# Ten instead of eight of sixteen k-tiles by seven products in the input projection of a decoder block

## The chip, the cores and the metric

The kernel runs on one core of a Trainium2 chip. The metric is the device time of one execution in microseconds. The kernel before takes 1338.32 us, the median of three runs (1338.11 to 1338.59).

## What is computed

One layer of a decoder for 256 rows of width 2048 in float32: a norm, one input projection, three kinds of causal attention over its q, k and v columns, three sigmoid gates, a branch projection, an output projection and a residual; then a second norm and a SwiGLU feed-forward part. Only the input projection is changed:

```python
h = rmsnorm(x, g_mix)                       # 256 x 2048
proj = h @ w_in                             # 2048 x 12288
qkv = proj[..., :3 * MIX_WIDTH]             # MIX_WIDTH = 2048: q, k, v
gates = jax.nn.sigmoid(proj[..., 3 * MIX_WIDTH:])   # three gates of 2048
...
merged = gates[0] * (o_a @ w_branch_a) + gates[1] * (o_b @ w_branch_b) + gates[2] * (o_c @ w_branch_c)
x = x + merged @ w_out
gu = rmsnorm(x, g_ffn) @ w_gu
x = x + (silu(gu[..., :D_FF]) * gu[..., D_FF:]) @ w_down
```

## The kernel before

**Three passes.** To keep float32's accuracy every factor is split into a rounded high part (type float32r) and the rest, its low part. `split` (L107 to L112) does this with a cast on ScalarE and a subtraction on VectorE. `product` (L169 to L174) multiplies with three matmuls: high by high (L172), high by low (L173), low by high (L174).

**Tiles.** The 256 rows are two halves t = 0 and 1 of 128. The 2048 inner columns are sixteen k-tiles of 128; four k-tiles make a chunk. Output columns come in blocks of 512. A weight block as it is loaded is 128 partitions x 2 k-tiles x 512 columns, 512 KB. One matmul covers one k-tile, one row half and 512 output columns.

**Units.** The projection's 24 column blocks are worked in units (L858): v block 0 and one gate block by the plain way (`project`), then eleven pairs of two column blocks A and B: four qk pairs, one vv, one vg and five gates pairs. Each pair is one call of `project_pair` (L351 to L424). In the text they are numbered 1 to 11.

**Seven products.** Chunks 0 and 1 (`WC`, eight k-tiles) are worked by a Strassen scheme with seven products in place of eight. The row halves and the halves of the chunk's k-tiles make the 2 x 2 blocks of the activations; the halves of the k-tiles (kh) and the columns A and B make those of the weights: b11 and b12 are the upper halves of A and B, b21 and b22 the lower ones. Forms 1, 2, 5, 6, 7, 3 and 4 are the seven products, summed into the PSUM tiles X, Y, Z and V. Sums of activations (forms 3, 5, 6, 7) are made once, by `sums_of_h`; `Both` holds them and hands out the operands. Sums of weights are made in each pair: u = b11 + b12 for form 5, then + b22 for form 6, then + b21 for form 4, and b12 + b22 for form 7. Some are VectorE additions (L344, `add_into` L333), some are DMAs issued on GpSimd that add into their target (L389, L395). With `by_dma`, in pairs 1 to 9, b12 + b22 is done by DMA; in pairs 10 and 11 VectorE does it.

**The plain rest.** The other eight k-tiles (chunks 2 and 3) are worked by `rest`: one 512 KB weight block, split, against both row halves, 12 matmuls. The list `ks` holds the four first k-tiles 8, 10, 12 and 14 of these blocks; each is used once for B (n = 1, into Z and V) and once for A (n = 0, into Y and X).

The order in a pair is forms 1, 2 and 5; two plain blocks of B; form 6; a plain block; form 7; a plain block; form 3; two plain blocks of A; form 4; two plain blocks; then the first splits of the next pair (`begin_pair`, L338). Seven forms of 12 matmuls and eight plain blocks of 12 make 180 matmuls. The snapshots s1, z5, x2 and x3 (L328) and the sums c22, c12 and c11 (L407, L408, L411, L423) put the outputs together.

**Buffers and order.** Split weights live in five slots each for high and low parts (`w_hi`, `w_lo` in the pool `wpool`). Raw blocks for forms live in the pool `gx` (`g_raw`, six slots), those for plain blocks in `w_raw` (four slots). Half-size tiles of 512 columns (`half_kb`) come from twelve slots `sc`. All weight loads are issued on SyncE in the order of the program (`fetch`). The tile framework orders the rest within each engine. With each split `parts` moves pending attention work on by a step (`advance`), so attention's instructions lie between those of the pairs. The last column block of the output projection and the gate-and-up projection go through `project_pair` too, with eight k-tiles by seven products.

Of the kernel before, what the change touches and what calls it, by code (L numbers as in the profile page):

```python
# [9 lines left out]
F32 = mybir.dt.float32  # L10
F32R = mybir.dt.float32r
# [7 lines left out]
P = 128  # L19
# [36 lines left out]
def hybrid_block(ctx: ExitStack, tc: tile.TileContext, x, w_in, w_branch, w_out, w_gu, w_down, rel_bias,  # L56
# [237 lines left out]
    class Both(Sums):  # L294


        def __init__(self, pl, cols, wc):
            super().__init__(pl, "b", wc, False)
            self.shared(pl)
            self.plain = cols.plain  # L300


    WC = (0, 1)

    def load(w, k, col0, pl=None):

        raw = pl.tile([P, 2, NB], F32, name="g_raw", bufs=6 if pl is gx else 4) if pl else wpool.tile([P, 2, NB], F32, name="w_raw", bufs=4)
        (nc.sync.dma_start if w is w_down else fetch)(raw, block(w, k, col0))
        return raw
# [16 lines left out]
    def snapshot(ps):  # L326
        sb = half_kb()
        nc.scalar.copy(sb, ps)  # L328
        return sb
# [5 lines left out]
    def quarter(acts, w, kh, col0):  # L335
        return [load(w, 4 * c + 2 * kh, col0, gx) for c in acts.wc]

    def begin_pair(acts, w, colA, colB):  # L338

        b11, b12 = (quarter(acts, w, 0, col0) for col0 in (colA, colB))  # L340
        p11 = [parts(b) for b in b11]
        u = [gx.tile([P, 2, NB], F32, name="u") for _ in acts.wc]
        for a, b, d in zip(b11, b12, u):
            nc.vector.tensor_add(d, a, b)  # L344
        b21 = quarter(acts, w, 1, colA)
        return p11, b12, u, b21, [parts(b) for b in (u if by_banks(w) else b21)]

    def by_banks(w):
        return w is w_gu or w is w_out

    def project_pair(acts, w, colA, colB, begun=None, nxt=None, by_dma=False, early=None):  # L351
# [6 lines left out]

        def form(ps, f, srcs, start, stop, split=False):
            for i, c in enumerate(acts.wc):  # L360
                wh, wl = srcs[i] if split else parts(srcs[i])
                for j in range(2):
                    product(ps, *acts.form(f, c, j), wh[:, j], wl[:, j], start and i + j == 0,
                            stop and i + j == len(acts.wc))

# [5 lines left out]

        ks = [k for c in range(KT // 4) if c not in acts.wc for k in (4 * c, 4 * c + 2)]
        p11, b12, u, b21, second = begun or begin_pair(acts, w, colA, colB)
        form(X, 1, p11, True, True, True)
        if by_banks(w):
            tc.keep_in_program_order(nc.scalar.copy(Y, X))
            form(Z, 5, second, True, True, True)
            doubled[:] = [tc.keep_in_program_order(nc.scalar.copy(V, Z))]
            form(Y, 2, b21, False, False)
        else:  # L380
            s1 = snapshot(X)
            form(Y, 2, second, True, False, True)
            form(Z, 5, u, True, True)
            z5 = snapshot(Z)
        plain = [load(w, k, colB) for k in ks[:2]]
        b22 = quarter(acts, w, 1, colB)
        if by_dma:
            for d, a in zip(b12, b22):
                nc.gpsimd.dma_start(d, a, accum_op=ALU.add)  # L389
        rest(1, ks[0], Z, V, start=not by_banks(w), raw=plain[0])  # L390
        rest(1, ks[1], Z, V, raw=plain[1])
        add_into(u, b22)
        form(X, 6, u, False, True)
        for d, a in zip(u, b21):
            nc.gpsimd.dma_start(d, a, accum_op=ALU.add)  # L395
        x2 = snapshot(X)
        rest(1, ks[2], Z, V)
        if not by_dma:
            add_into(b12, b22)
        form(X, 7, b12, False, True)  # L400
        x3 = snapshot(X)
        rest(1, ks[3], Z, V, stop=True)
        c22 = half_kb()
        if by_banks(w):
            nc.vector.tensor_sub(c22, V, x3)
        else:
            nc.vector.tensor_sub(z5, z5, x3)  # L407
            nc.vector.tensor_add(c22, V, z5)  # L408
        form(Z, 3, b22, False, True)
        c12 = half_kb()  # L410
# [3 lines left out]
        for k in ks[:2]:  # L414
            rest(0, k, Y, X)
        form(X, 4, u, False, False)
        for k in ks[2:]:
# [62 lines left out]
    for c in range(2, 4):  # L480
        whole[c] = gx.tile([P, NT, 4, P], F32, name="g_raw", bufs=6)
    columns = {c: [whole[c][:, t] for t in range(NT)] for c in range(4)}
# [103 lines left out]
    def load_rows():  # L586
        for t in range(NT):
            for n in range(2):
                rows.append(gx.tile([P, 2 * NB], F32, name="g_raw", bufs=6))
                fetch(rows[-1], x[t * P:(t + 1) * P, 2 * n * NB:2 * (n + 1) * NB])  # L590
                yield
# [297 lines left out]
    for (kind, what), after in zip(units, units[1:] + [(None, None)]):  # L889
# [46 lines left out]

    pgx.close()
    tc.keep_in_program_order(nc.scalar.preload_act_table_set("natural_log_exp_and_others"))
    m = Columns(pool(pm, "pm", "right"), "m", KT)
# [371 lines left out]
```

## Time and profile before

| | |
|---|---|
| median of three runs | 1338.32 us |
| the profiled execution | 1337.34 us |
| its span in the profile | 1335.6 us |
| DMA engines, mean | 266 GB/s |
| w_raw blocks of the input projection | 103 loads of 512 KB, 7.0 us to land |
| g_raw blocks of the input projection | 88 loads of 512 KB, 6.2 us to land |

The engines: PE is TensorE's matmuls, PEld its weight loads, DVE is VectorE, ACT ScalarE, POOL GpSimd, SP SyncE. Lines of the kernel are given as L108. A row of a timeline reads: start, duration, engine, line, operation, output and inputs with their shapes, number. In a table of windows each row has the stretch, its length, and for each engine busy time and the number of instructions, then the granted clock of TensorE, the share of the DMA engines and what they moved. A row of DMA issues ends with the KB of one and the median time from issue to landing. Windows of a pair are cut where VectorE starts c11 (L423), the last sum of a pair.

### The profile page before, as it was taken

Reading aid. Unit: us, or ns where it says so; the run is one execution under the profiler, and the core shown is the slowest. Engines: PE = TensorE matmul, PEld = TensorE weight load, DVE = VectorE, ACT = ScalarE, POOL = GpSimd, SP = SyncE. Lnnn points to the kernel's source line nnn. Section 1 sums busy time; section 2 is a strip of 40 time slices with the busy share of each in tenths; the row PEclk is TensorE's granted clock in tenths of the full one; section 3 lists DMA queues with packets and bytes.
Section 4 is the critical chain, followed back from the end, with each engine's and each line's share of the span. In section 5 each row is a group of like instructions: output and inputs, shape, how many; then the busy total and the mean of one; then the engine's idle time right before and its main releaser. Section 6 shows DMA issues by size and latency. Waiting matters only on the chain.

```text
span 1335.6 us, 17783 instructions
## 1 busy us (share of the span) xinstructions
PE 1328.6 (99%) x6243; PEld 1158.7 (87%) x6243; DVE 1168.9 (88%) x1254; ACT 940.9 (70%) x1209; POOL 130.9 (10%) x195
## 2 busy tenths in 40 slices
PE   9999999999999999999999999999999999999998
PEld 6888888888888888888888888888888888888887
DVE  7978898989888897986999999989899997998887
ACT  7786867788777776544777778777877875665563
POOL 1100110001111111100210000001000001001010
PEclk9999999999999999999999999999999999999999
DMA  9997878797788878877988889889899977789883
GB/s 359 308 282 246 263 210 258 252 277 223 263 267 282 277 241 289 294 249 244 305 312 267 259 265 278 238 252 308 279 286 274 281 216 253 252 276 301 270 271 96
DMA packets 119505, 354.70 MB, mean 266 GB/s; under 512 B 32832, under 2 KB 34552, under 8 KB 119416
## 3 DMA queue, kind: packets, MB, share of 16 engines
q1 hardware_dynamic: 77016, 277.45, 58.4%
q0 software_dynamic: 19984, 69.76, 22.2%
q10 hardware_dynamic: 22416, 6.36, 2.8%
q8 instruction: 49, 0.80, 0.2%
q14 instruction: 40, 0.33, 0.1%
HBM read 294.26 MB, written 14.70 MB: 231 GB/s over the span
## 4 chain that ended last, share of the span: by engine, by line
PE 98%; DMA 1%; ACT 0%; DVE 0%; SPq 0%; issue 0%; DVEq 0%
PE qs L172 12%; PE ps L173 12%; PE qs L174 12%; PE qs L173 12%; PE ps L174 12%; PE ps L172 12%; PE z L173 4%; PE z L172 4%; PE z L174 4%; PE v L172 2%; PE v L173 2%; PE v L174 2%; PE tr L174 1%; PE tr L172 1%; PE tr L173 1%; PE tr L205 1%
## 5 line engine op out<-in xcount | busy, mean ns | idle before, releaser
L108 DVE TENSOR_TENSOR w_lo<-w_raw,w_hi 128x1024 fp32r<-128x1024 f32 x302 | 366.0, 1220 | 57.9 <-ACT w_hi L108 56.6
L108 ACT CAST w_hi<-w_raw 128x1024 fp32r<-128x1024 f32 x302 | 313.7, 1047 | 111.3 <-PE qs L174 39.5
L108 ACT CAST w_hi<-g_raw 128x1024 fp32r<-128x1024 f32 x216 | 222.8, 1050 | 106.0 <-PE qs L174 32.9
L108 DVE TENSOR_TENSOR w_lo<-g_raw,w_hi 128x1024 fp32r<-128x1024 f32 x216 | 257.5, 1220 | 19.7 <-ACT w_hi L108 17.4
L108 ACT CAST w_hi<-u 128x1024 fp32r<-128x1024 f32 x162 | 168.7, 1049 | 107.1 <-PE qs L174 22.4
L108 DVE TENSOR_TENSOR w_lo<-u,w_hi 128x1024 fp32r<-128x1024 f32 x162 | 195.6, 1221 | 42.5 <-ACT w_hi L108 37.6
L173 PE MATMUL ps<-w_lo,h_hi 128*128 128x512 f32 x352 | 134.0, 381 | 0.5 <-DVE w_lo L108 0.5
L174 PE MATMUL ps<-w_hi,h_lo 128*128 128x512 f32 x352 | 133.5, 380 | 0.1
L172 PE MATMUL ps<-w_hi,h_hi 128*128 128x512 f32 x352 | 129.1, 382 | 0.0
L173 PE MATMUL qs<-w_lo,h_hi 128*128 128x512 f32 x332 | 126.5, 381 | 0.0
L174 PE MATMUL qs<-w_hi,h_lo 128*128 128x512 f32 x332 | 126.0, 380 | 0.0
L172 PE MATMUL qs<-w_hi,h_hi 128*128 128x512 f32 x332 | 121.3, 382 | 0.0
L173 PEld LDWEIGHTS ps<-w_lo,h_hi 128*128 128x128 f32 x352 | 66.5, 189 | 10.4 <-DVE w_lo L108 1.3
L174 PEld LDWEIGHTS ps<-w_hi,h_lo 128*128 128x128 f32 x352 | 66.5, 189 | 10.3 <-DVE h_lo L108 1.1
L395 POOL DMA_DIRECT2D u<-g_raw x46 | 40.1, 871 | 360.1 <-DVE w_lo L108 299.6
L172 PEld LDWEIGHTS ps<-w_hi,h_hi 128*128 128x128 f32 x352 | 66.3, 189 | 9.5 <-ACT h_hi L108 0.3
L172 PEld LDWEIGHTS qs<-w_hi,h_hi 128*128 128x128 f32 x332 | 62.7, 189 | 9.1 <-ACT sc L328 0.4
L173 PEld LDWEIGHTS qs<-w_lo,h_hi 128*128 128x128 f32 x332 | 62.8, 189 | 8.7
L174 PEld LDWEIGHTS qs<-w_hi,h_lo 128*128 128x128 f32 x332 | 62.8, 189 | 8.7
L344 DVE TENSOR_TENSOR u<-g_raw 128x1024 f32<-128x1024 f32 x46 | 56.0, 1219 | 13.1 <-DMA g_raw<-in_w_gu 9.5
L333 DVE TENSOR_TENSOR u<-u,g_raw 128x1024 f32<-128x1024 f32 x46 | 54.2, 1218 | 0.0
L389 POOL DMA_DIRECT2D g_raw<-g_raw x20 | 17.3, 867 | 252.2 <-DMA g_raw<-in_w_in 133.7
(440 smaller groups left out, 2977.2 us busy)
## 6 DMA issues: line engine op xcount, KB each, us to landing
w_raw<-in_w_in SPq DMA_DIRECT2D x103, 512.0 KB, 7.0
g_raw<-in_w_in SPq DMA_DIRECT2D x88, 512.0 KB, 6.2
g_raw<-in_w_gu SPq DMA_DIRECT2D x88, 512.0 KB, 6.2
w_raw<-in_w_gu SPq DMA_DIRECT2D x88, 512.0 KB, 6.4
w_raw<-in_w_down SPq DMA_DIRECT2D x56, 512.0 KB, 4.8
u<-g_raw POOLq DMA_DIRECT2D x50, 512.0 KB, 6.6
w_raw<-in_w_branch SPq DMA_DIRECT2D x32, 512.0 KB, 4.6
g_raw<-in_w_down SPq DMA_DIRECT2D x32, 512.0 KB, 5.0
```

The source lines that it names most:

```text
L108: cast, rest = nc.scalar.copy(hi, src), nc.vector.tensor_sub(lo, src, hi.bitcast(F32))
L172: nc.tensor.matmul(ps, ah, wh, start=start, stop=False, **how)
L173: nc.tensor.matmul(ps, ah, wl, start=False, stop=False, **how)
L174: nc.tensor.matmul(ps, al, wh, start=False, stop=stop, **how)
L205: nc.tensor.transpose(pt[:, i, :], src[:, i * P:(i + 1) * P], ident)
L333: tc.keep_in_program_order(nc.vector.tensor_add(d, d, a))
L344: nc.vector.tensor_add(d, a, b)
L389: nc.gpsimd.dma_start(d, a, accum_op=ALU.add)
L395: nc.gpsimd.dma_start(d, a, accum_op=ALU.add)
```

## The change

Each pair of the input projection takes half a chunk more by seven products: k-tiles 8 and 9, one for each kh. Of `ks` three blocks remain (10, 12, 14), each still used for A and B.

- `put_half` (new, called once after the plain gate unit) makes the sums of activations for k-tiles 8 and 9 with four operations on 128 x 128 and two splits. They are kept in columns of `h` that no form and no plain block reads any more (`spare`).
- `begin_half` (new) loads the full blocks a and b (k-tiles 8 and 9 of A and B), splits a, and adds u = a's upper + b's upper half. a's two halves serve forms 1 and 2.
- Every form gets one more half-chunk product of three matmuls (`more`). For forms 5, 6 and 4 u is split anew as half a block (`parts_of_half`, in a full slot of `w_hi` and `w_lo`): first as it is, then with b's lower half added by VectorE, then with a's lower half added by DMA. For forms 7 and 3 b is split once as a whole (`hq`), after its lower half was added to its upper half, by DMA in pairs 1 to 9 and by VectorE in pairs 10 and 11.
- A plain block of B between forms 7 and 3 and one of A at the pair's end are gone.
- `g_raw` gets eight slots, not six, until the input projection ends.

```diff
+        def spare(self, t):
+            return [x[:, t:8:4, P:S] for x in (self.cols.hi, self.cols.lo)]
+
+        def put_half(self, k, t0, t1):
+            self.half = k
+            a11, a12, a21, a22 = (a[:, kh:kh + 1, :] for a in (t0, t1) for kh in range(2))
+            nc.vector.tensor_sub(a22, a21, a22)
+            nc.vector.tensor_sub(a21, a11, a21)
+            nc.vector.tensor_sub(a11, a22, a11)
+            nc.vector.tensor_add(a12, a12, a11)
+            for t, a in enumerate((t0, t1)):
+                split(*self.spare(t), a)
+
+        def form_half(self, f):
+            if f in SUM_AT:
+                kh, t = SUM_AT[f]
+                return [x[:, 4 * kh + t, P:S] for x in (self.cols.hi, self.cols.lo)]
+            return self.plain(*{1: (0, self.half), 2: (0, self.half + 1), 4: (1, self.half + 1)}[f])
...
+    raw_bufs = [8]
...
+    def parts_of_half(src):
+        hi, lo = (wpool.tile([P, 2, NB], F32R, name=f"w_{n}")[:, 0] for n in ("hi", "lo"))
+        split(hi, lo, src)
+        return hi, lo
+
+    def begin_half(acts, w, colA, colB):
+        a, b = (load(w, acts.half, col0, gx) for col0 in (colA, colB))
+        pa_ = parts(a)
+        u = half_kb()
+        nc.vector.tensor_add(u, a[:, 0], b[:, 0])
+        return a, b, pa_, u
+
     def begin_pair(acts, w, colA, colB):
         b11, b12 = (quarter(acts, w, 0, col0) for col0 in (colA, colB))
         p11 = [parts(b) for b in b11]
+        half = begin_half(acts, w, colA, colB) if getattr(acts, "half", None) else None
...
                     product(ps, *acts.form(f, c, j), wh[:, j], wl[:, j], start and i + j == 0,
-                            stop and i + j == len(acts.wc))
+                            stop and not more and i + j == len(acts.wc))
+            if more:
+                product(ps, *acts.form_half(f), *more, False, stop)
...
+        if half:
+            ha, hb, hp, hu = half
+            ks.remove(acts.half)
+        form(X, 1, p11, True, True, True, half and half_of(hp, 0))
...
+            form(Y, 2, second, True, False, True, half and half_of(hp, 1))
+            form(Z, 5, u, True, True, more=half and parts_of_half(hu))
...
+            if half:
+                nc.gpsimd.dma_start(hb[:, 0], hb[:, 1], accum_op=ALU.add)
...
         add_into(u, b22)
-        form(X, 6, u, False, True)
+        if half:
+            nc.vector.tensor_add(hu, hu, hb[:, 1])
+        form(X, 6, u, False, True, more=half and parts_of_half(hu))
         for d, a in zip(u, b21):
             nc.gpsimd.dma_start(d, a, accum_op=ALU.add)
+        if half:
+            nc.gpsimd.dma_start(hu, ha[:, 1], accum_op=ALU.add)
         x2 = snapshot(X)
-        rest(1, ks[2], Z, V)
+        rest(1, ks[2], Z, V, stop=len(ks) == 3)
         if not by_dma:
             add_into(b12, b22)
-        form(X, 7, b12, False, True)
+            if half:
+                nc.vector.tensor_add(hb[:, 0], hb[:, 0], hb[:, 1])
+        hq = parts(hb) if half else None
+        form(X, 7, b12, False, True, more=half and half_of(hq, 0))
         x3 = snapshot(X)
-        rest(1, ks[3], Z, V, stop=True)
+        for k in ks[3:]:
+            rest(1, k, Z, V, stop=True)
...
-        form(Z, 3, b22, False, True)
+        form(Z, 3, b22, False, True, more=half and half_of(hq, 1))
...
-        form(X, 4, u, False, False)
+        form(X, 4, u, False, False, more=half and parts_of_half(hu))
...
+            if kind == "gate":
+                hs.put_half(8, *(a[:, 0:2] for a in columns[2]))
             ahead = begin_pair(*nxt) if nxt else None
```

More of the change, by code (lines that the diff above doesn't have):

```diff
@@ L299, in __init__ @@
             self.shared(pl)
-            self.plain = cols.plain
+            self.plain, self.cols, self.half = cols.plain, cols, None
+        def spare(self, t):
[14 more added lines that the diff above has]
+            return self.plain(*{1: (0, self.half), 2: (0, self.half + 1), 4: (1, self.half + 1)}[f])
     WC = (0, 1)
+    raw_bufs = [8]
     def load(w, k, col0, pl=None):
-        raw = pl.tile([P, 2, NB], F32, name="g_raw", bufs=6 if pl is gx else 4) if pl else wpool.tile([P, 2, NB], F32, name="w_raw", bufs=4)
+        raw = pl.tile([P, 2, NB], F32, name="g_raw", bufs=raw_bufs[0] if pl is gx else 4) if pl else wpool.tile([P, 2, NB], F32, name="w_raw", bufs=4)
         (nc.sync.dma_start if w is w_down else fetch)(raw, block(w, k, col0))
@@ L345, in begin_pair @@
         b21 = quarter(acts, w, 1, colA)
-        return p11, b12, u, b21, [parts(b) for b in (u if by_banks(w) else b21)]
+        return half, p11, b12, u, b21, [parts(b) for b in (u if by_banks(w) else b21)]
     def by_banks(w):
@@ L357, in project_pair, with form @@
         Z, V = others()
-        def form(ps, f, srcs, start, stop, split=False):
+        def form(ps, f, srcs, start, stop, split=False, more=None):
             for i, c in enumerate(acts.wc):
@@ L363, in form, with half_of @@
                     product(ps, *acts.form(f, c, j), wh[:, j], wl[:, j], start and i + j == 0,
-                            stop and i + j == len(acts.wc))
+                            stop and not more and i + j == len(acts.wc))
+            if more:
+                product(ps, *acts.form_half(f), *more, False, stop)
+        def half_of(p, j):
+            return [x[:, j] for x in p]
         def rest(n, k, p0, p1, start=False, stop=False, raw=None):
@@ L372, in project_pair @@
         ks = [k for c in range(KT // 4) if c not in acts.wc for k in (4 * c, 4 * c + 2)]
-        p11, b12, u, b21, second = begun or begin_pair(acts, w, colA, colB)
-        form(X, 1, p11, True, True, True)
+        half, p11, b12, u, b21, second = begun or begin_pair(acts, w, colA, colB)
+        if half:
+            ha, hb, hp, hu = half
+            ks.remove(acts.half)
+        form(X, 1, p11, True, True, True, half and half_of(hp, 0))
         if by_banks(w):
@@ L381, in project_pair @@
             s1 = snapshot(X)
-            form(Y, 2, second, True, False, True)
-            form(Z, 5, u, True, True)
+            form(Y, 2, second, True, False, True, half and half_of(hp, 1))
+            form(Z, 5, u, True, True, more=half and parts_of_half(hu))
             z5 = snapshot(Z)
@@ L480, in hybrid_block @@
     for c in range(2, 4):
-        whole[c] = gx.tile([P, NT, 4, P], F32, name="g_raw", bufs=6)
+        whole[c] = gx.tile([P, NT, 4, P], F32, name="g_raw", bufs=raw_bufs[0])
     columns = {c: [whole[c][:, t] for t in range(NT)] for c in range(4)}
@@ L588, in load_rows @@
             for n in range(2):
-                rows.append(gx.tile([P, 2 * NB], F32, name="g_raw", bufs=6))
+                rows.append(gx.tile([P, 2 * NB], F32, name="g_raw", bufs=raw_bufs[0]))
                 fetch(rows[-1], x[t * P:(t + 1) * P, 2 * n * NB:2 * (n + 1) * NB])
@@ L937, in hybrid_block @@
     pgx.close()
+    raw_bufs[0] = 6
     tc.keep_in_program_order(nc.scalar.preload_act_table_set("natural_log_exp_and_others"))
```

## The prediction, made before the changed kernel ran

> **What bounds the kernel now.** I read the busy table and the chain first, then cut the input projection into its eleven pairs (one window from the end of one pair to the end of the next), and compared TensorE with the engine nearest behind it.
>
> ```profile
> span 1335.6 us, 17783 instructions
> ## 1 busy us (share of the span) xinstructions
> PE 1328.6 (99%) x6243; PEld 1158.7 (87%) x6243; DVE 1168.9 (88%) x1254; ACT 940.9 (70%) x1209; POOL 130.9 (10%) x195
> ```
>
> ```profile
> PE 98%; DMA 1%; ACT 0%; DVE 0%; SPq 0%; issue 0%; DVEq 0%
> ```
>
> TensorE is busy for 1328.6 of 1335.6 us and is 98% of the chain that ended last. So a matmul that disappears shortens the kernel by its issue interval, as long as TensorE is still fed without a gap. Whether it is fed is decided inside the pairs. In the next table each row is one pair in order (pairs 1 to 11); the first number behind the window is its length, then come the busy times.
>
> ```profile
> core 0: us, PE busy (x) PEld busy (x) DVE busy (x) ACT busy (x) POOL busy (x), PEclk, DMA share, GB/s
> 52.00:90.50 38.50, 38.50 (x180) 33.72 (x179) 32.73 (x35) 29.37 (x33) 4.64 (x6) 1.00 0.92 284
> 90.50:134.20 43.70, 43.70 (x214) 38.08 (x213) 36.94 (x38) 32.03 (x39) 4.08 (x5) 1.00 0.81 249
> 134.20:177.70 43.50, 43.50 (x207) 37.91 (x206) 37.16 (x45) 35.87 (x72) 2.80 (x4) 1.00 0.77 234
> 177.70:223.60 45.90, 45.90 (x230) 40.10 (x229) 39.52 (x49) 30.07 (x42) 5.05 (x6) 1.00 0.84 255
> 223.60:263.80 40.20, 40.20 (x192) 35.29 (x192) 36.10 (x47) 33.30 (x74) 3.33 (x4) 1.00 0.81 246
> 263.80:309.70 45.90, 45.90 (x229) 40.40 (x228) 42.44 (x61) 36.72 (x78) 5.00 (x6) 1.00 0.82 249
> 309.70:354.20 44.50, 44.50 (x225) 38.93 (x224) 39.91 (x52) 34.27 (x54) 5.31 (x7) 1.00 0.78 248
> 354.20:397.00 42.80, 42.80 (x209) 37.57 (x208) 35.84 (x41) 32.84 (x46) 5.67 (x8) 1.00 0.87 275
> 397.00:437.10 40.10, 40.10 (x189) 35.19 (x188) 32.95 (x30) 28.69 (x32) 4.84 (x7) 1.00 0.90 284
> 437.10:476.50 39.40, 39.40 (x184) 34.16 (x183) 37.02 (x35) 28.57 (x33) 3.99 (x6) 1.00 0.79 265
> 476.50:515.00 38.50, 38.50 (x180) 33.72 (x179) 33.91 (x32) 28.34 (x32) 5.12 (x8) 1.00 0.76 237
> ```
>
> TensorE fills every window at a granted clock of 1.00. A pair alone is 180 matmuls (pairs 1 and 11); what the others have on top is attention. VectorE is second, with an idle rest of only 2.38 us in pair 10 (39.40 less 37.02) and 3.46 in pair 6 (45.90 less 42.44). These two columns decide the case.
>
> **What TensorE gains.** Two k-tiles against two row halves and two column blocks cost 2 x 2 x 2 x 3 = 24 matmuls by the plain way. By seven products of one k-tile each they cost 7 x 3 = 21. So three matmuls go per pair, 33 in eleven pairs.
>
> ```profile
> 101.77 0.38 PE L173 MATMUL ps<-w_lo,h_hi 128*128 128x512 f32 x1
> ...
> 104.58 0.38 PE L174 MATMUL ps<-w_hi,h_lo 128*128 128x512 f32 x1
> ```
>
> Between these two rows lie 13 steps of back-to-back matmuls: 2.81 / 13 = 0.216 us each (the 0.38 is the pipelined length, not the interval). The gain is 33 x 0.216 = 7.1 us, 0.65 us a pair.
>
> **What VectorE pays.** The two plain weight blocks that go (k-tiles 8 and 9 of each column block) took two full splits; the two blocks that come, a and b in full width, take two as well. On top come three splits of half a block (the sum u for forms 5, 6 and 4) and two half-width additions (u itself, and u plus the lower half of b). In pairs 10 and 11, which do not add by DMA, there is a third (b's upper half).
>
> ```profile
> 458.80 1.22 DVE L108 TENSOR_TENSOR w_lo<-w_raw,w_hi 128x1024 fp32r<-128x1024 f32 x1
> 459.93 0.68 DVE L407 TENSOR_TENSOR sc<-sc 128x512 f32<-128x512 f32 x1
> 460.53 1.22 DVE L108 TENSOR_TENSOR w_lo<-w_raw,w_hi 128x1024 fp32r<-128x1024 f32 x1
> 461.67 0.68 DVE L408 TENSOR_TENSOR sc<-v,sc 128x512 f32<-128x512 f32 x1
> ```
>
> From start to start a full operation takes 1.13 to 1.14 us and a half one 0.60, less than their lengths, since one begins before the other has ended. So a pair costs VectorE 5 x 0.60 = 3.0 us more (3.6 in pairs 10 and 11), while TensorE's time shrinks by 0.65. VectorE's idle rest falls by 3.65 us a pair, by 4.25 in the last two. By the table it becomes: 2.1, 3.1, 2.7, 2.7, **0.45**, **-0.19**, **0.94**, 3.3, 3.5, **-1.87**, **0.34** us.
>
> The Trainium skill (VectorE: DVE Perf Modes, section "The DRAIN you can't avoid") says that the next operation does not start until the pipe of the one before has emptied. By that rule each new half operation would cost at least its 0.68 us, 0.4 more a pair, the negative rests would grow from 2.1 to about 3 us, and the forecast would come out about 1 us later; the rows above, with starts 0.60 apart, speak against it.
>
> How much rest is enough? The gate-and-up stage works in the same seven forms:
>
> ```profile
> 686.40:727.10 40.70, 40.70 (x193) 35.40 (x192) 38.66 (x48) 31.61 (x40) 2.30 (x3) 1.00 0.87 290
> 727.10:768.00 40.90, 40.90 (x191) 35.83 (x190) 38.18 (x36) 32.29 (x37) 1.71 (x2) 1.00 0.81 244
> ```
>
> There TensorE has no gap with 2.04 and 2.72 us of rest. So pairs 1 to 4, 8 and 9 should stay fed. Pairs 5, 6, 7, 10 and 11 fall below anything the trace shows.
>
> **What the shortage costs.** Lower bound: nothing, if the split weights that lie ready carry each pair over. It cannot go below nothing, because TensorE has no gap to lose. Upper bound: every pair needs 2.04 us of rest, and TensorE waits for what is missing: 1.59 + 2.23 + 1.10 + 3.91 + 1.70 = 10.5 us. The leads of the tightest places narrow this. Each pair of rows is the split that is needed first and the first matmul that reads it.
>
> ```profile
> 453.01 1.23 DVE L108 TENSOR_TENSOR w_lo<-g_raw,w_hi 128x1024 fp32r<-128x1024 f32 x1
> ```
>
> ```profile
> 456.56 0.38 PE L173 MATMUL qs<-w_lo,hi 128*128 128x512 f32 x1
> ```
>
> ```profile
> 492.16 1.23 DVE L108 TENSOR_TENSOR w_lo<-g_raw,w_hi 128x1024 fp32r<-128x1024 f32 x1
> ```
>
> ```profile
> 494.98 0.38 PE L173 MATMUL ps<-w_lo,hi 128*128 128x512 f32 x1
> ```
>
> ```profile
> 245.55 1.23 DVE L108 TENSOR_TENSOR w_lo<-g_raw,w_hi 128x1024 fp32r<-128x1024 f32 x1 [0.76 <-ACT w_hi L108]
> ```
>
> ```profile
> 248.71 0.38 PE L173 MATMUL qs<-w_lo,hi 128*128 128x512 f32 x1
> ```
>
> Form 7 of pairs 10 and 11 (first two pairs of rows) has its weights 2.3 and 1.6 us ahead. Up to there VectorE gets two full splits more (a's and the whole b's) and five half operations, 2 x 1.14 + 5 x 0.60 = 5.28 us, and TensorE 12 half-chunk matmuls, 2.59 us: the lead falls by 2.7, to -0.4 and -1.1 us. Form 3 of pair 5 (last two) has 1.9 us. Up to there VectorE gets 5.28 - 0.60 (b is added by DMA) - 1.14 (the plain block that stood in between) = 3.54 us, TensorE 15 matmuls more and 12 fewer, 0.65 us: the lead falls to -1.0. That is 2.5 us of stalls. Pair 10 is short by 1.87 us over its whole length and form 7 shows only 0.4 of it; I count the remaining 1.5 in full, since pair 11 behind it has no rest to pay it back. **Stalls: 4.0 us**, between 0 and 10.5.
>
> **What is hidden.** ScalarE gets three half casts a pair; its rest is nowhere under 6.9 us (pair 5), so at even the 0.68 us of a VectorE half operation they fit. The sums for the half chunk before pair 1 are four subtractions or additions of 128 columns and two splits of 256, each shorter than a 512-column one: under 6 x 0.60 = 3.6 us, in a gate unit where VectorE rests 4.07:
>
> ```profile
> 26.00:52.00 26.00, 26.00 (x122) 22.78 (x121) 21.93 (x31) 20.42 (x30) 0.00 (x0) 1.00 0.89 339
> ```
>
> Without that cover they would cost up to 3.6 us once. On the queues, POOL gets two accumulating DMAs more a pair (one in the last two), each half the size of these:
>
> ```profile
> q0 software_dynamic: 19984, 69.76, 22.2%
> u<-g_raw POOLq DMA_DIRECT2D x50, 512.0 KB, 6.6
> ```
>
> The one into u waits for form 6's split and is needed by form 4. Forms 7 and 3 and three plain blocks lie between, 15 + 15 + 36 matmuls, 14 us against 6.6 to land; behind it in POOL's queue stand gate stores, which nobody waits for at once. 22.2% of the span for 69.76 MB is 4.25 us of all sixteen engines per MB, so 0.52 MB add 2.2 us a pair: pair 1, the fullest, goes from 0.92 x 38.5 = 35.4 to 37.6 of its 37.85 us. It just fits. The loads are as many as before, b21's two stand behind a and b in SP's order, and two more raw buffers let them start earlier.
>
> **Sum.** Against the profiled execution: 1337.34 - 7.1 + 4.0 = 1334.2 us. The median shown lies 0.98 above that execution, so 1338.32 - 7.1 + 4.0 = **1335.2 us**.
>
> **Rivals.**
> - *Fully fed.* The leads carry the thin pairs. For it: in nearly all pairs VectorE rests in the trace, and it can move its attention work. Against it: pair 10 is over 100%. Time 1338.3 - 7.1 = 1331.2. Chance 0.20.
> - *The gain is eaten.* All five thin pairs stall for their missing rest, 1338.3 - 7.1 + 10.5 = 1341.7; anything from 1338 up belongs here. For it: pairs 5 to 7 would run VectorE at about 99% for 129 us. Against it: a buffer of several splits stands ahead of TensorE. Chance 0.20.
> - *Slower, by buffers.* There are five slots for split weights, and the block for forms 7 and 3 is split before form 7 and held until form 3 has ended. If slots are given out in turn, the first plain block behind form 3 can only be cast then. TensorE would wait for one cast and one split, 1.1 + 1.1 us, in each pair: 11 x 2.2 = 24 us, so 1338.3 - 7.1 + 4.0 + 24 = 1359. It decides as soon as a slot must wait for its own turn; if any free slot is taken, four others remain and it vanishes. Before, tiles are freed in the order of their use, so the trace cannot tell which holds. Chance 0.12. The Trainium skill (Perfetto Trace Analysis, section "Optimization Strategy") reads the same gap repeating on an engine that should be saturated as a sign of too little room for the next tile; this would be such a gap.
>
> That the forms don't add up to 33 matmuls fewer is not open: the count follows from the loops.
>
> **How the numbers follow.** Forecast 0.48, fully fed 0.20, eaten 0.20, slower 0.12. The range 1331.0 to 1342.0 reaches from no stall to all of the shortage and leaves out the last rival. A measurement here tells 0.2%, 2.7 us, from no change: faster means under 1335.6, slower over 1341.0. The forecast case, 1333 to 1338, gives a bit over half to faster (0.28) and 0.20 to same; with the fully fed case faster has 0.48. Of the eaten case 0.15 is same and 0.05 slower: same 0.35, slower 0.17.
>
> **What would show it.** 33 matmuls fewer on TensorE. In the windows of pairs 1 to 4, 8 and 9 no gap and 0.65 us less each; in pairs 5 to 7 and 10 and 11 VectorE busy for nearly the whole window and TensorE waiting on VectorE's splits, most at form 7 of pairs 10 and 11. I am wrong if the wait repeats in every pair at one place (buffers), if TensorE waits on DMA, or if the thin pairs show no wait.

## The result and the profile after

The changed kernel takes **1350.44 us** (median of five runs, 1349.32 to 1353.4) against 1338.2 us of the kernel before beside it (five runs, 1337.44 to 1338.59): ratio 1.0096, 95% interval 1.0081 to 1.0110. It is slower by 12.2 us. The forecast was 1335.2, faster by 3.1, with a range of 1331 to 1342: wrong in sign and outside the range.

The busy table and the chain of the profile after:

```profile
span 1347.4 us, 17856 instructions
PE 1328.7 (99%) x6210; PEld 1150.6 (85%) x6210; DVE 1200.9 (89%) x1317; ACT 960.4 (71%) x1244; POOL 147.7 (11%) x215
```

```profile
PE 73%; DVE 12%; issue 6%; DMA 5%; ACT 2%; POOL 1%; SPq 0%; DVEq 0%; POOLq 0%; ACTq 0%
```

The 33 matmuls are gone (6243 to 6210), yet TensorE's busy time is what it was. A row of a matmul is 0.38 us long while matmuls start 0.216 apart, so one that starts up to 0.16 us late leaves no gap between the rows, and that time counts as busy. The chain tells more. It was 98% TensorE and is now 73%; VectorE holds 12%, and DMA, ScalarE and "issue" 13% together.

The input projection by pairs again (pairs 4, 5, 10 and 11; start and end, length, then busy times and numbers of instructions):

```profile
core 0: us, PE busy (x) PEld busy (x) DVE busy (x) ACT busy (x) POOL busy (x), PEclk, DMA share, GB/s
180.70:229.50 48.80, 46.13 (x229) 38.82 (x228) 45.25 (x65) 33.11 (x53) 6.72 (x8) 1.00 0.79 237
229.50:270.10 40.60, 40.60 (x190) 35.45 (x188) 36.19 (x43) 34.59 (x72) 5.10 (x6) 1.00 0.89 272
...
446.40:489.80 43.40, 40.61 (x184) 34.02 (x183) 40.25 (x41) 32.08 (x38) 5.41 (x8) 1.00 0.79 256
489.80:526.50 36.70, 36.37 (x165) 30.78 (x165) 35.85 (x36) 27.12 (x31) 5.46 (x8) 1.00 0.71 218
```

TensorE no longer fills them. How much of attention falls into a window shifts, so lengths of windows don't compare; instead I took the time of the last matmul of each pair that reads the low part of the weights, before and after. By it pair 1 loses 1.2 us, pairs 2 and 3 nothing, pair 4 loses 4.0, pairs 6 to 8 lose 0.5, 0.9 and 0.9, pairs 9, 10 and 11 lose 1.6, 1.9 and 1.6; pair 5 gains 1.3. Without stalls each would gain 0.65.

What TensorE waits for in the eleven pairs (total us, times, longest; the two largest of five rows); the same view of before has no row at all here:

```profile
PE qs L173 <- DVE w_lo L108: 4.9, 5, 1.6
PE ps L173 <- DVE w_lo L108: 4.5, 7, 1.8
```

So TensorE waits for VectorE's splits. And one thing VectorE waits for, at the border from pair 10 to 11 (timeline of VectorE, then of TensorE; the bracket is the idle time before and what ended it):

```profile
472.34 0.69 DVE L463 TENSOR_TENSOR sc<-z,sc 128x512 f32<-128x512 f32 x1
476.14 0.69 DVE L368 TENSOR_TENSOR sc<-g_raw 128x512 f32<-128x512 f32 x1 [3.11 <-DMA g_raw<-in_w_in]
476.75 2.35 DVE L108 TENSOR_TENSOR w_lo<-u,w_hi 128x1024 fp32r<-128x1024 f32 x2
```

```profile
478.02 0.48 PE L173 MATMUL qs<-w_lo,h_hi 128*128 128x512 f32 x1 [1.09 <-DVE w_lo L108]
```

L368 is the half sum of the *next* pair, a's upper half plus b's. In VectorE's order it stands ahead of the two splits for *this* pair's form 4 (the third row). The load of b is late, VectorE stands 3.1 us, and the split that TensorE needs next stands behind it: the first of the two, 1.22 us long, is done at 477.97, and the matmul goes at 478.02. The same happens at 83.08 (4.1 us of waiting) and at 437.27 (2.9 us, with a plain block's split behind it): 12.3 us in five places, the other two 1.6 and 0.6 us.

### The profile page after: what moved, and what is told of

The parts are those of the page before. It is cut to its first block, busy times and chain, and to the rows that moved or that the text cites. A ratio compares the mean times of both kernels' runs of the same rounds, so it can differ in the third digit from the quotient of the medians.

```text
span 1347.4 us, 17856 instructions
## 1 busy us (share of the span) xinstructions
PE 1328.7 (99%) x6210; PEld 1150.6 (85%) x6210; DVE 1200.9 (89%) x1317; ACT 960.4 (71%) x1244; POOL 147.7 (11%) x215
## 4 chain that ended last, share of the span: by engine, by line
PE 73%; DVE 12%; issue 6%; DMA 5%; ACT 2%; POOL 1%; SPq 0%; DVEq 0%; POOLq 0%; ACTq 0%
PE ps L173 9%; PE qs L173 8%; PE ps L174 8%; PE qs L174 8%; PE ps L172 8%; PE qs L172 8%; DVE w_lo L108 7%; PE z L172 4%; PE z L173 4%; PE z L174 4%; DMA g_raw<-in_w_in 3%; PE v L172 2%; PE v L174 2%; PE v L173 2%; DMA u<-g_raw 2%
## 5 line engine op out<-in xcount | busy, mean ns | idle before, releaser
L108 DVE TENSOR_TENSOR w_lo<-w_raw,w_hi 128x1024 fp32r<-128x1024 f32 x280 | 339.1, 1221 | 48.5 <-ACT w_hi L108 45.9
L108 ACT CAST w_hi<-w_raw 128x1024 fp32r<-128x1024 f32 x280 | 290.2, 1048 | 112.5 <-PE qs L174 42.3
L108 ACT CAST w_hi<-g_raw 128x1024 fp32r<-128x1024 f32 x238 | 245.0, 1049 | 107.7 <-PE qs L174 29.7
L108 DVE TENSOR_TENSOR w_lo<-g_raw,w_hi 128x1024 fp32r<-128x1024 f32 x238 | 282.6, 1222 | 12.1 <-ACT w_hi L108 9.9
L108 DVE TENSOR_TENSOR w_lo<-u,w_hi 128x1024 fp32r<-128x1024 f32 x162 | 195.1, 1222 | 26.9 <-ACT w_hi L108 24.6
L378 DVE TENSOR_TENSOR u<-g_raw 128x1024 f32<-128x1024 f32 x46 | 55.9, 1221 | 12.3 <-DMA g_raw<-in_w_gu 7.7
L173 PE MATMUL qs<-w_lo,hi 128*128 128x512 f32 x108 | 41.9, 388 | 2.4 <-DVE w_lo L108 2.4
```

What stands on the lines that cost most here:

```text
L108: cast, rest = nc.scalar.copy(hi, src), nc.vector.tensor_sub(lo, src, hi.bitcast(F32))
L173: nc.tensor.matmul(ps, ah, wl, start=False, stop=False, **how)
```

## The experiments

Times are medians, ratios are against the kernel before, run beside it on the same chip. Two causes were in question from the start: the mere amount of VectorE's new work (the prediction's own term), and the order and the buffers in which it stands.

### VectorE's work alone

**e1** puts half-size subtractions that nobody reads into the kernel before, where the change has its half operations: five a pair, six in the last two (at forms 1, 5, 6, 4 and, in the last two, 7).

```diff
+    def vector_work(w, a, b):
+        if w is w_in:
+            nc.vector.tensor_sub(half_kb(), a[:, 0], b[:, 0])
...
+            vector_work(w, *u)
```

> The kernel before with five more VectorE subtractions of 128x512 in each pair of the input projection (six in the last two) whose results nobody reads; TensorE's work, the slots and the loads are as before. Theory W (VectorE's added work alone starves TensorE): 11 to 19 us slower than before, about 1350 to 1357 us. Theory O (the half blocks are split ahead of a form's own blocks and hold slots of split weights) and theory D (VectorE stands behind the half sum that waits for a late load): within 4 us of before, 1338 to 1342 us.

Measured: 1343.84 us, ratio 1.0051 (1.0034 to 1.0067): VectorE's work alone costs 6.2 us here, where the 33 matmuls are still made. The prediction had 4.0. It lies between the two expectations: the work is part of the loss and not all of it.

**e4** keeps the seven products and the matmuls, but forms 5, 6 and 4 read a block of their own in place of u, so no half split of u and no half sum is made (form 5 is shown, forms 6 and 4 are alike). a and b are still split, and b's halves are still added.

```diff
-            form(Z, 5, u, True, True, more=half and parts_of_half(hu))
+            form(Z, 5, u, True, True, more=half and "own")
```

> The changed kernel without the half sums: the half-chunk products of forms 5, 6 and 4 read the split of the form's last own block instead. Left out are the three half splits, the two half additions on VectorE and the DMA into u, so the output is not the reference's; TensorE keeps its 33 matmuls fewer, and a's and b's loads and the splits that forms 1, 2, 7 and 3 hold stay. Theories W, O and D all put the loss into what is left out: 1331 to 1333 us. If it stays above 1338 us, the loss lies in what is kept (the two held slots, the loads).

Measured: 1337.93 us, 1.0001 (0.9991 to 1.0010). It takes the whole loss away, but stays 7 us above what 33 matmuls fewer would give. **e8** goes further: all half products read a block of their own; a and b are only loaded and added.

```diff
-        form(X, 7, b12, False, True, more=half and half_of(hq, 0))
+        form(X, 7, b12, False, True, more=half and "own")
```

> The changed kernel with none of the half chunk's splits and sums: every half-chunk product reads the split of its form's last own block. Left out are a's and b's splits, the half splits and half additions and the DMA into u; a and b are still loaded, so VectorE has 2 x 1.14 us less a pair than before the change and no slot of split weights is held. The output is not the reference's. Theory S, slots of split weights (a's and b's splits hold one slot each through two forms): 1331 to 1333 us. If late loads and raw buffers are the cause: 1335 us or more, as the loads are as many and in the same order.

Measured: 1336.98 us, 0.9990 (0.9980 to 0.9999). Still no 1331. What VectorE waits for in the pairs, of e4 and of e8:

```profile
DVE g_raw L445 <- DMA g_raw<-in_w_in: 8.6, 2, 4.7
```

```profile
DVE g_raw L448 <- DMA g_raw<-in_w_in: 9.2, 2, 5.7
```

With the work nearly gone, VectorE stands for the load of b all the same, now at the addition of b's halves for pairs 10 and 11. In e8 the longer of these waits delays TensorE. The addition stands ahead of a split that pair 9 still needs:

```profile
423.11 0.69 DVE L448 TENSOR_TENSOR g_raw<-g_raw 128x512 f32<-128x512 f32 x1 [5.71 <-DMA g_raw<-in_w_in]
423.71 1.22 DVE L108 TENSOR_TENSOR w_lo<-w_raw,w_hi 128x1024 fp32r<-128x1024 f32 x1
```

This split is done at 424.93, and TensorE, which waited 1.95 us for it, goes on at 424.99 (the row stands in the last section). Pair 9 loses 3.4 us by it, where it should gain 0.65: 4.0 of the 5.9 us that e8 lacks to 1331. So where VectorE asks for b is a cost of its own, beside the work.

### Where the half operations stand

**e2** makes each half split behind its form's own splits, not ahead. In the change `more=parts_of_half(hu)` is worked out before the form begins, so the half split is issued first, though its product is the form's last.

```diff
-                product(ps, *acts.form_half(f), *more, False, stop)
+                product(ps, *acts.form_half(f), *(more() if callable(more) else more), False, stop)
...
-            form(Z, 5, u, True, True, more=half and parts_of_half(hu))
+            form(Z, 5, u, True, True, more=half and (lambda: parts_of_half(hu)))
```

> The changed kernel with one edit: in forms 5, 6 and 4 the half block is split after the form's two own blocks, not ahead of them. Theory O: 6 us or more faster than the changed kernel, 1344 us or less. Theories W and D: within 2 us of it, 1348 to 1352 us.

Measured: 1351.6 us, 1.0108 (1.0093 to 1.0123): no help. VectorE still waits 9.4 us at the half sum.

**e3** moves the half sum instead, from the pair's beginning to just before form 5; the half split stays ahead.

```diff
-        u = half_kb()
-        nc.vector.tensor_add(u, a[:, 0], b[:, 0])
-        return a, b, pa_, u
+        return a, b, pa_, half_kb()
...
+                nc.vector.tensor_add(hu, ha[:, 0], hb[:, 0])
             form(Z, 5, u, True, True, more=half and parts_of_half(hu))
```

> The changed kernel with one edit: the half sum u = a + b is no longer made on VectorE at the end of the pair before, but just ahead of form 5, so that VectorE has no reason to stand waiting for b's load. Theory D: 5 us or more faster than the changed kernel, 1345 us or less, and the 12.3 us of waiting for the load gone. Theories W and O: within 2 us of it.

Measured: 1360.02 us, 1.0173 (1.0158 to 1.0188): worse than the change by 9.6. The wait for b's load is gone, and VectorE waits more for ScalarE's casts (18.3 us in the change to the end of pair 11):

```profile
DVE w_lo L108 <- ACT w_hi L108: 33.6, 43, 3.0
```

A sum, its cast and its half split follow each other at once, ahead of form 5's own splits. But this row alone shows no price: in the kernel before it is 46.1 us, and TensorE has no gap. The largest single loss of e3 lies elsewhere. Pair 8 loses 6.9 us (0.9 in the change), where VectorE stands for ScalarE's part of attention and TensorE for VectorE's:

```profile
377.65 0.18 DVE L786 RECIPROCAL sm_st<-sm_st 128x4 f32<-128x4 f32 x1 [7.75 <-ACT p L785]
```

```profile
378.82 0.45 PE L795 MATMUL tr<-ident,p 128*128 128x128 f32 x1 [4.58 <-DVE p L788]
```

So 6.0 of the 9.6 us lie in attention's steps of this one pair, and e3 says little on the half sum. Neither edit helps by itself; that told nothing yet about the two together.

**e5** gives the half additions to GpSimd (one of the three is shown).

```diff
-        nc.vector.tensor_add(u, a[:, 0], b[:, 0])
+        nc.gpsimd.tensor_add(u, a[:, 0], b[:, 0])
```

> The changed kernel with the half additions (u, u plus b's lower half, and b's upper half in the last two pairs) on GpSimd instead of VectorE. Theory W (VectorE's work): 24 operations of 0.60 us less on a VectorE that is short, 14 us at most, so 3 to 8 us faster than the changed kernel, 1342 to 1347 us. Theory D (VectorE stands waiting for b's load): the 12.3 us of that wait go too, 1342 us or less. Theory S (slots and raw buffers that the half chunk holds): within 3 us of the changed kernel. Worse than it if a GpSimd addition slows VectorE beside it or holds up the DMAs queued behind it.

Measured: 1350.85 us, 1.0094 (1.0079 to 1.0109): no gain, though VectorE waits for no load. The groups point at two reasons, neither tried by itself: GpSimd's half sum (minimum, median and maximum in ns), then the splits of u on VectorE in the change and in e5 (busy, mean ns of one):

```profile
L368 POOL TENSOR_TENSOR sc<-g_raw x11: 1283/1942/10589, 49.2 to 481.1; 128x512 f32<-128x512 f32 x11
```

```profile
L108 DVE TENSOR_TENSOR w_lo<-u,w_hi 128x1024 fp32r<-128x1024 f32 x162 | 195.1, 1222 | 26.9 <-ACT w_hi L108 24.6
```

```profile
L108 DVE TENSOR_TENSOR w_lo<-u,w_hi 128x1024 fp32r<-128x1024 f32 x162 | 200.9, 1258 | 30.7 <-ACT w_hi L108 28.8
```

The addition takes 1.9 us in the median against 0.69 on VectorE, and VectorE's splits grow from 1222 to 1258 ns. The Trainium skill (GPSIMD Engine Reference, sections "4.1 Engine selection" and "8. Key points") calls two-input additions there about twice as slow and names contention with VectorE's instructions that read two inputs; the direction agrees, and the measured addition is 2.8 times as long.

### Slots

**e6** splits the three halves of u into two half-size scratch tiles each, rather than into a full slot of `w_hi` and `w_lo`.

```diff
-        hi, lo = (wpool.tile([P, 2, NB], F32R, name=f"w_{n}")[:, 0] for n in ("hi", "lo"))
+        hi, lo = (half_kb(F32R) for _ in range(2))
```

> The changed kernel with the three half splits of a pair in two of the twelve half-size slots each, not in the five full slots of split weights. Theory S, as far as the slots of split weights carry it: 4 us or more faster than the changed kernel, 1346 us or less. Theories W and D: within 2 us of it.

Measured: **1339.31 us**, 1.0010 (1.0000 to 1.0020): 11.1 us back with one line. The border from pair 10 to 11 on VectorE:

```profile
468.04 1.22 DVE L108 TENSOR_TENSOR w_lo<-u,w_hi 128x1024 fp32r<-128x1024 f32 x1
469.17 1.22 DVE L108 TENSOR_TENSOR o_lo<-o_raw,o_hi 128x1024 fp32r<-128x1024 f32 x1
470.31 1.21 DVE L108 TENSOR_TENSOR w_lo<-w_raw,w_hi 128x1024 fp32r<-128x1024 f32 x1
471.44 0.68 DVE L108 TENSOR_TENSOR sc<-sc 128x512 fp32r<-128x512 f32 x1
472.05 0.68 DVE L368 TENSOR_TENSOR sc<-g_raw 128x512 f32<-128x512 f32 x1
```

Two things changed at once. Five full slots are free for full blocks; and the tile framework now puts form 4's splits (and here a plain block's and the half split) *ahead* of the next pair's half sum, which waits 1.5 us in all, not 12.3. Which of the two was worth the 11 us?

**e9** splits a and b into scratch halves as well.

```diff
-        pa_ = parts(a)
+        pa_ = in_halves(a)
...
-        hq = parts(hb) if half else None
+        hq = in_halves(hb) if half else None
```

> The changed kernel with every split of the half chunk in half-size slots: besides the three half splits of u also a and b, each split as two halves, so that nothing of the half chunk takes one of the five full slots. Theory S: the slots of a and b cost too, so faster than the kernel with u's halves alone moved (1339.3): 1333 to 1337 us. Theory W: two half splits in place of one full one cost VectorE 2 x 0.06 us more a pair, so 1339 to 1341 us.

Measured: 1343.19 us, 1.0034 (1.0022 to 1.0047), 3.9 worse than e6, and outside both expectations. VectorE has more half operations, and more halves share the twelve half-size slots; which of the two costs was not tried. The gain of free full slots doesn't go on. **e11** gives a sixth slot to the full kernel, paid for with two raw blocks of `g_raw` (six), one of `w_raw` (three) and one `sc`.

```diff
-    wpool = pool(ctx, "wpool", "right", 5)
-    scratch = pool(ctx, "scratch", "right", 12)
+    wpool = pool(ctx, "wpool", "right", 6)
+    scratch = pool(ctx, "scratch", "right", 11)
...
-    raw_bufs = [8]
+    raw_bufs = [6]
```

> The changed kernel with six slots of split weights in place of five, paid for by raw buffers (six and later five for forms, three for plain blocks) and one half-size slot, which slow the later stages; only the input projection's end is read. Theory S: it ends at 516 us or less in the trace (526 us in the changed kernel, 515 before), although the raw buffers are fewer. Theories W and D: 524 us or more.

Measured: 1685.05 us, 1.2592. It says nothing about slots: six raw blocks starve every pair (what VectorE waits for):

```profile
DVE u L354 <- DMA g_raw<-in_w_in: 145.1, 21, 8.4
```

**e13** and **e14** repeat it with its own control. Both have `w_raw` at three and `sc` at ten; e14 alone has the sixth slot (the last two lines).

```diff
-    scratch = pool(ctx, "scratch", "right", 12)
+    scratch = pool(ctx, "scratch", "right", 10)
...
-    wpool = pool(ctx, "wpool", "right", 5)
+    wpool = pool(ctx, "wpool", "right", 6)
```

> The changed kernel with five slots of split weights as it has them, and three slots for plain raw blocks (four before) and ten half-size slots (twelve before): the control for the next kernel, which needs that room. No theory says by how much the smaller pools slow it; the input projection ends at 526 us or later in the trace (526 in the changed kernel).

> The same small pools with six slots of split weights. Theory S (the half blocks take slots that TensorE needs as cover): the input projection ends 6 us or more before that of the control with five slots. Theory W (VectorE's work is the limit, and moving the half blocks only gave another order): within 2 us of the control.

Measured: control 1366.47 us, 1.0211 (1.0192 to 1.0229); six slots 1364.86 us, 1.0198 (1.0180 to 1.0217). Each has two runs, over 3 us apart, so the medians don't separate them; the traces are read instead. At the end of pair 11 the sixth slot has gained 3.7 us (23.1 against 19.4 us behind the kernel before). That is between the two expectations. It is one execution of each, and 1.7 us of it were there before pair 1 began (its first matmul goes at 56.82 and 55.15 us). The wait at the half sum remained, in the control and in e14:

```profile
DVE sc L368 <- DMA g_raw<-in_w_in: 15.4, 7, 4.9
```

```profile
DVE sc L368 <- DMA g_raw<-in_w_in: 12.4, 7, 3.6
```

### The wait without the slots

**e16** keeps the full slots and takes the wait away: the half sum is tied behind the last split that form 2 needs, and the half splits come last in their forms, as in e2.

```diff
+        second = [parts(b) for b in (u if by_banks(w) else b21)]
+        if half:
+            with tc.issue_after(split_last[1].ins):
+                nc.vector.tensor_add(half[3], half[0][:, 0], half[1][:, 0])
...
+            form(Z, 5, u, True, True, more=half and (lambda: parts_of_half(hu)))
```

> The changed kernel with its full split slots, but VectorE takes the half sum of a and b only behind the last split that forms 1 and 2 need, and each half split follows its form's own blocks. So VectorE should hardly stand for b's load there (under 2 us in all, 12.3 in the changed kernel), and no half split is asked for before its sum is ready. Theory W (the wait of VectorE for b's load is the price of the 11 us that the scratch slots gave back): 1338 to 1342 us. Theory S (the full slots that the half blocks hold are the price, and the wait for the load is only a symptom of them): no gain, 1347 to 1353 us, and VectorE's idle time in the eleven pairs stays near 39 us, with splits waiting for their casts in place of the load.

Measured: 1342.49 us, 1.0033 (1.0022 to 1.0045): 8.0 us back, and no row of a wait for b's load is left. Theory W's window reached to 1342, theory S began at 1347, and VectorE's idle time does not stay near 39 us (33.6, below): the order carries most of the gain. From e2 to e16 the half sum alone moves, and the time falls from 1351.6 to 1342.5, 9.1 us, with e2's 9.4 us of waiting gone. Whether the half sum's new place would do without e2's move was not run. **e17** was to bring the wait back into e6 by loading b behind b21.

```diff
         b21 = quarter(acts, w, 1, colA)
+        if half:
+            half[1] = load(w, acts.half, colB, gx)
+            nc.vector.tensor_add(half[3], half[0][:, 0], half[1][:, 0])
```

> The version with half splits in scratch slots (1339.3), but b is loaded behind the four blocks b11, b12 and the two b21 rather than ahead of b21, so that the half sum, which still stands ahead of b21's splits on VectorE, has to wait for a later load. Theory W: the wait of VectorE at the half sum comes back (8 us or more in all) and with it the time, 1345 to 1352 us. Theory S: the slots are free, the wait may come back but costs under 3 us: 1338 to 1342 us.

Measured: 1339.64 us, 1.0008 (0.9999 to 1.0017), and the half sum waits 1.7 us. The wait didn't come back, so this test tells nothing about its price, and nothing here puts the wait back into a kernel that lacks it; it shows that a load two blocks later is early enough where the sum stands behind form 4's splits.

The eleven pairs as one window each, from 52 us to the end of pair 11, of the kernel before, the change, e1, e6 and e16:

```profile
52.00:515.00 463.00, 463.00 (x2223) 405.08 (x2222) 404.52 (x453) 350.07 (x530) 49.84 (x66) 1.00 0.82 257
```

```profile
52.00:526.50 474.50, 462.60 (x2190) 396.97 (x2189) 435.43 (x512) 368.91 (x564) 66.97 (x86) 1.00 0.86 260
```

```profile
52.00:520.90 468.90, 465.43 (x2226) 404.51 (x2226) 434.10 (x511) 350.82 (x530) 50.01 (x66) 1.00 0.81 253
```

```profile
52.00:517.40 465.40, 460.04 (x2196) 399.89 (x2196) 435.90 (x514) 366.27 (x565) 67.07 (x86) 1.00 0.88 267
```

```profile
52.00:520.50 468.50, 460.82 (x2193) 398.62 (x2192) 434.87 (x511) 367.50 (x564) 67.54 (x86) 1.00 0.87 263
```

The third busy column is VectorE: 404.5 us before, 434 to 436 in the other four. Its idle time (length less busy) is 58.5 before and 39.1 in the change, 34.8 in e1, 33.6 in e16, 29.5 in e6. From the change to e6 VectorE does the same work, idles 9.6 us less, and the pairs are 9.1 us shorter; to e16 it idles 5.4 less and they are 6.0 shorter. So with 435 us of work VectorE's standing is paid for nearly in full. With 404.5 us of work it was not: the kernel before has the most idle time and no gap on TensorE.

### Fewer pairs with the half chunk

**e7** leaves the half chunk out of pairs 10 and 11 (`hs9` is the scheme without it); **e10** does so in e6; **e15** is e6 with it in pairs 1, 2, 3, 5, 8 and 9 only; **e12** is e6 with e5's edit, the half additions on GpSimd. The first line is that of e7 and e10, the line behind the dots that of e15.

```diff
+        hs = hs9 if kind == "gates" and what[0] in (chunks[8], chunks[10]) else hs8
...
+    thin = [units[i] for i in (5, 7, 8, 11, 12)]
+        hs = hs9 if (kind, what) in thin else hs8
```

> The changed kernel with the half chunk in pairs 1 to 9 alone; pairs 10 and 11 are worked as before. If the loss sits above all where VectorE also adds b's upper half and splits the attention output: the 3.9 us lost in these two pairs go, 1346 us. Theory W: pairs 1 to 9 still lose about 7 us, so not under 1344 us.

> The half splits in half-size slots, and the half chunk in pairs 1 to 9 alone. Theory W says that what is left is VectorE's shortage in the thin pairs; pairs 10 and 11 lost 0.9 and 2.5 us against 0.65 us of gain each, so 1336 to 1338 us. If the rest lies elsewhere (loads, pairs 4 to 7): 1339 us or more.

> The half splits in half-size slots, and the half chunk only in the pairs where the kernel with it in all eleven gained (1, 2, 3, 5, 8 and 9); pairs 4, 6, 7, 10 and 11 as before. Theory W (what is left is VectorE's shortage in the thin pairs): six times 0.65 us less than before, 1334 to 1335 us. If the remaining loss moves with the attention work into other pairs: 1336 to 1339 us.

> The half splits in half-size slots and the half additions on GpSimd. With the slots out of the way theory W expects the 24 additions (14 us of VectorE) to show now: 1334 to 1337 us. If it stays at 1338 us or more, VectorE's work in the half additions is not what is left, or GpSimd gives it back.

Measured: e7 1345.12 us, 1.0050 (1.0035 to 1.0065), so the last two pairs cost 5.3 us of the change; e10 1337.31 us, 0.9994 (0.9985 to 1.0003); e15 1337.47 us, 0.9993 (0.9984 to 1.0002); e12 1343.48 us, 1.0039 (1.0025 to 1.0053), 4.2 worse than e6: on GpSimd the additions cost more than VectorE saves. The best versions, e10 and e15, equal the kernel before; none beats it.

## Why the prediction was wrong, point by point

**33 matmuls, 7.1 us: right.** In e6, where few stalls are left, pairs 1 to 3 gain 0.65, 0.64 and 0.65 us.

**VectorE's work: the price of an operation nearly right, the stalls mis-sized and partly mis-read.** VectorE's busy time grew by 30.9 us (404.52 to 435.43) where 11 x 3.0 + 1.2 = 34.2 was counted. The stalls of this alone were put at 4.0 us and are 6.2 in e1. One part of the difference is a slip: the three matmuls that the prediction quoted as the first to read the split weights read the block's *second* k-tile. The first ones stand three matmuls earlier (pairs 10, 11 and 5):

```profile
455.92 0.38 PE L173 MATMUL qs<-w_lo,hi 128*128 128x512 f32 x1
```

```profile
494.34 0.38 PE L173 MATMUL ps<-w_lo,hi 128*128 128x512 f32 x1
```

```profile
248.06 0.38 PE L173 MATMUL qs<-w_lo,hi 128*128 128x512 f32 x1
```

By these the leads are 1.7, 0.95 and 1.3 us, 0.64 less each, and the same working gives stalls of 1.0 + 1.75 + 1.6 = 4.35 us, with the 0.9 of pair 10's shortage that is then left 5.2 us: near e1's 6.2 in size. The places differ, though: in e1 pairs 2, 4 and 11 lose 1.3, 2.2 and 1.7 us, pair 5 loses 0.9 and pair 10 nothing, so the nearness is partly luck. Where the larger waits are out of the way, the predicted place shows as predicted. Form 7 of pair 10 in e16 (the high-by-high matmul, then the one that waits):

```profile
461.01 0.38 PE L172 MATMUL qs<-w_hi,hi 128*128 128x512 f32 x1
462.35 0.48 PE L173 MATMUL qs<-w_lo,hi 128*128 128x512 f32 x1 [0.96 <-DVE w_lo L108]
```

In the changed kernel itself pairs 10 and 11 stall earlier, at the border, and form 7 has no such gap. Pair 5, for which 1.0 us was counted, has no gap either (busy 40.60 of 40.60 us).

**Pairs 1 to 4, 8 and 9 stay fed: wrong.** The rest of a whole window doesn't say where it lies. In pair 4 four multiplications of attention stand directly ahead of form 6's splits (VectorE, then TensorE, in the changed kernel):

```profile
191.35 2.50 DVE L831 TENSOR_TENSOR sc<-sc,rr 128x512 f32<-128x512 f32 x4
193.76 2.37 DVE L108 TENSOR_TENSOR w_lo<-u,w_hi 128x1024 fp32r<-128x1024 f32 x2
```

```profile
195.04 0.48 PE L173 MATMUL qs<-w_lo,hi 128*128 128x512 f32 x1 [1.62 <-DVE w_lo L108]
```

Two matmuls also start 1.92 us apart at 85 us (pair 1, behind L368), and 1.26 and 2.19 us apart at 410 and 442 us (pair 9), where 0.22 is normal. So these pairs hold stalls that the forecast excluded. The gate-and-up stage with its 2.04 us of rest was no measure for them.

**"The loads are as many as before ... two more raw buffers let them start earlier": this is the step that failed.** From it the prediction took that b is there when VectorE asks for it, and put VectorE's wait for loads at nothing. In the changed kernel VectorE waits 12.3 us for b at the half sum, and in its order splits that TensorE needs sooner stand behind that sum. Moving the sum alone, from e2 to e16, took 9.1 us off; moving it and the half splits, from the change to e16, took off 8.0.

An earlier start was not enough. At the border from pair 10 to 11 the first load goes 24.5 us ahead of the pair's last low-part matmul, 18.8 before the change. But b is the sixth of the eight blocks that are issued there in a row. It is issued at 469.49 and lands 6.6 us later, just before L368 starts at 476.14, while L368's place in VectorE's order comes 3.1 us sooner.

A raw block comes free only when its last reader has finished. Ten blocks a pair now go through eight slots (before eight through six), and the last reader of a, like that of b21, is an accumulating DMA on POOL's queue. What SP's queue waited for before it could issue a load, in the pairs, before and after:

```profile
SPq L105 <- DMA u<-g_raw: 8.6, 8, 1.7
```

```profile
SPq L105 <- DMA sc<-g_raw: 69.7, 10, 8.5
SPq L105 <- DMA u<-g_raw: 48.3, 20, 5.2
```

8.6 us became 118. Yet all waits of SP's queue in the pairs come to 386 us before and 398 after, since those for VectorE's splits fell from 325.6 to 233.1; and in e6 these two rows sum to 119.6, with 1.5 us of waiting at the half sum. So the loads now wait for other readers, but that this made b late is not shown. The prediction listed every new operation of VectorE by its length and counted how many stand ahead of forms 7 and 3; it asked for none of them what it has to wait for.

**The rival "slower, by buffers" (0.12): right in sign, not in mechanism.** No wait repeats in every pair at the first plain block behind form 3. "Fully fed" is excluded by TensorE's waits. "The gain is eaten" (0.20) has the right sign, but its 1341.7 rests on at most 10.5 us of stalls from VectorE's shortage; all stalls come to 12.2 + 7.1 = 19.3 us, and e1 has 6.2 of that kind.

**The sum.** -7.1 (matmuls) + 6.2 (VectorE's work, e1) + 8.0 (the wait for b, the change less e16) = +7.1, of 12.2 measured. Of the other 5.1 us, 3.2 is what e6 gains over e16. Whether that is the slots that the half splits take or once more the order is not shown: e14's sixth slot gained 3.7, but among scarcer buffers and 1.7 of it ahead of the pairs. The last 1.9 stays open. The terms need not add up either, since e1's work was put into the kernel before.

## What to carry to other kernels

When work moves to an engine that has little rest, place each new instruction in that engine's order and ask what it waits for and what is queued behind it; the sum of durations can be the smaller half of the price (here 6.2 of 19.3 us of stalls). An addition that prepares the next round belongs behind the last operation that the present round still needs. When a lead is read off a trace, look for the first reader of the tile, not the first row that looks like it, and when you ask when a load can start, look for the last reader of its buffer, DMAs included.

## What the runs showed of the hardware

After a short gap TensorE can fall to half its rate. In e8, after 2.33 us between two starts (matmuls normally start 0.216 apart):

```profile
422.66 0.38 PE L172 MATMUL ps<-w_hi,h_hi 128*128 128x512 f32 x1
424.99 0.70 PE L173 MATMUL ps<-w_lo,h_hi 128*128 128x512 f32 x1 [1.95 <-DVE w_lo L108]
425.48 0.63 PE L174 MATMUL ps<-w_hi,h_lo 128*128 128x512 f32 x1
425.91 0.63 PE L172 MATMUL ps<-w_hi,h_hi 128*128 128x512 f32 x1
...
428.47 0.41 PE L172 MATMUL ps<-w_hi,h_hi 128*128 128x512 f32 x1
```

Eight matmuls start 0.43 to 0.49 us apart until 428.47. The granted clock of TensorE in this stretch is 0.53 (the window, its length, TensorE's busy time, then the clock, the share of the DMA engines and GB/s):

```profile
424.90:428.50 3.60, 3.51 (x9) 0.53 1.04 422
```

So pair 9 lost 3.4 us by a wait of 1.95. The length of the gap alone does not decide. In e3 a wait of 1.16 us is followed by such a stretch (granted clock 0.52 from 425.4 to 428.6), in e7 one of 2.73 us is not (1.00 from 86.1 to 89.6):

```profile
424.90 0.48 PE L173 MATMUL qs<-w_lo,hi 128*128 128x512 f32 x1 [1.16 <-DVE w_lo L108]
```

```profile
86.12 0.48 PE L173 MATMUL ps<-w_lo,h_hi 128*128 128x512 f32 x1 [2.73 <-DVE w_lo L108]
```

The Trainium skill (TensorE: Matmul & The Clock Gate, section "Part 1: The HAM clock gate") says that the clock halves after an idle window of about 3.4 us and returns after a busy one of the same length. The slow stretch, 428.47 - 424.99 = 3.5 us, agrees; the gap ahead of it is shorter than the page's window, and here the measurement decides.
